# A two-layer decoder trunk on one core: the low part of two weight pairs per unit taken from DRAM twice by GpSimd's transfers

## The chip, the cores and the metric

One core of one Trainium2 chip runs the whole program in one launch. The metric is device time in microseconds (us) from start to end. Before the change the median of 3 runs is 2133.17 us (2133.06 to 2133.46). All data is float32.

## The reference

For 256 tokens of width 2048 and two layers:

```python
h = rms_norm(x, attn_norm)
proj = h @ w_in                 # columns: GLA q,k,v,gate, a rank-16 gate, attention q,k,v
o_gla = gla_chunked(...)        # gated linear attention, 8 heads
o_sb  = stick_breaking_attention(...)   # 8 heads, strictly causal
x = x + concat(o_gla, o_sb) @ w_o
hm = rms_norm(x, mlp_norm)
x = x + square(relu(hm @ w_up)) @ w_down        # hidden width 8192
```

Nearly all of the work is matrix products of the 256 tokens with float32 weights.

## The kernel before

TensorE multiplies in a rounded float32 format. To keep float32 precision each weight tile is split in two: `whi` is the weight rounded, `wlo` is what the rounding dropped. Operands are split in the same way, and a product is three matmuls of 128x512: high times `whi`, high times `wlo`, low times `whi` (`product`, L1112 to L1123).

The work of the projections is cut into **units**: 1024 output columns of one weight matrix, with 2048 input rows in eight **pairs** of 128-row blocks (0 to 7). A layer's list is `g` (gate columns), two `o`, then eight `up` and eight `down`; in between stand `iv`, `ik`, `iq`, three projections of the next layer, which also stand ahead of layer 0. 38 units are of the kinds `up`, `down`, `iv`, `ik`, `iq`. In such a unit there are three kinds of pair:

- **Fast pairs** (1, 3, 5, 6): a Strassen-like scheme, four steps of 6, 6, 6 and 3 matmuls (21 instead of 24), for which VectorE forms sums of weight blocks (`ts`, L840).
- **Plain pairs** (0, 4): two steps of 12 matmuls, each on one half tile of 128x1024. ScalarE copies `raw` to `whi` (L1008), VectorE subtracts to get `wlo` (L1012).
- **Added pairs** (2, 7): two steps of 12 matmuls. ScalarE makes `whi` (L1008) and also a rounded, negated copy `dlo` (L1018); then a transfer issued by GpSimd adds `raw` to `dlo` within SBUF (L1021), so that `dlo` holds the low part and VectorE does nothing. There are two `dlo` tiles.

All raw weights come by transfers issued on SyncE (`load`, L967 to L981) into five `raw` tiles of 1 MB that are used in turn (three named `raw`, two named `raw2`). There are five `whi` half tiles and four `wlo` half tiles, also used in turn, so the splitting runs four or five steps ahead of TensorE.

The order on TensorE, VectorE and ScalarE within these stretches is set by `Plan`: each piece of work has a length written in the code, a due time counted back from TensorE's order, and the pieces are placed by earliest due time. SyncE and GpSimd keep the order of the code. Code outside these stretches (the opening, and the attention of each layer) is ordered by the framework, which also decides where the first planned pieces stand among the code ahead of them.

At the opening, x comes in four blocks `xb`; each is turned by TensorE (L471) with the identity `ident` that GpSimd builds, scaled and split by ScalarE (L481) and VectorE (L487); then the first unit (value columns) runs with its own splitting (L575, L577) of loads at L564, and its matmuls are at L594 to L596. The attention uses the same code (L575, L594).

Of the kernel before, what the change touches and what calls it, by code (L numbers as in the profile page):

```python
# [17 lines left out]
P = 128  # L18
# [3 lines left out]
STEPS = [0, 0, 1, 1, 1, 2, 3, 1, 3, 2, 3, 3, 4, 4, 5, 5, 6, 5, 5, 6, 6, 6, 7, 7]  # L22
LOADS = [0, 1, 2, 3, 4, 5, 6, 7]
FAST = (1, 3, 5, 6)
FEWER = [0, 0, 1, 1, 1, 2, 3, 1, 3, 2, 3, 3, 4, 4, 5, 5, 6, 6, 6, 6, 7, 7], (1, 3, 6)
ADDED = (2, 7)
# [21 lines left out]
class Plan:  # L48
# [10 lines left out]
    class Piece:  # L59
        def __init__(self, engine, length, fn, deps, lag):  # L60
            self.engine, self.length, self.fn, self.lag = engine, length, fn, lag
            self.deps = deps
            self.users = []
            self.after = []
# [4 lines left out]
    def add(self, engine, length, fn, *deps, lag=0.0):  # L69
        flat = []  # L70
        for d in deps:
            flat.extend(d if isinstance(d, (list, tuple)) else [d])
        self.pieces.append(Plan.Piece(engine, length, fn, [d for d in flat if d], lag))
        return self.pieces[-1]

    def run(self):
# [25 lines left out]
        order, events, count = [], [], 0  # L102
        for p in self.pieces:
            if not p.deps:
                events.append((0.0, count, p))
                count += 1
        came = set()
        while events:
            now, _, p = heapq.heappop(events)
# [6 lines left out]
            for e in free:  # L116
                if free[e] > now + 1e-9:
                    continue
                if e in ready:
                    if not ready[e]:  # L120
                        continue
                    p = heapq.heappop(ready[e])[2]
# [6 lines left out]
                heapq.heappush(events, (free[e], count, None))  # L129
                count += 1  # L130
                for u in p.users:
# [4 lines left out]
                    if not left[u]:  # L136
                        heapq.heappush(events, (at[u], count, u))
# [9 lines left out]
def trunk_kernel(  # L147
# [59 lines left out]

    ATT = ("wg", "ident16", "mask16", "tri", "nones", "gmask", "reset", "v4", "lr", "lrT", "ha", "hh", "hl", "hA", "on", "dec", "S", "kdz", "row", "bc", "eg")
    MLP = ("whi5", "dlo", "sxh", "sx", "ts", "raw2")
# [213 lines left out]
    def forms(op, i, t, tag):  # L423

        keep = tag is None
# [16 lines left out]
        def high():  # L442
            if e:
                if keep:
# [378 lines left out]
    def ordered(l, units, hT, rst, ug, gates_t, mixed=None, ons=None):  # L823
# [11 lines left out]
        RING, LOWS, ADDS, RAWS = 5, 4, 2, 5  # L835
# [11 lines left out]
        def unit_order(u):  # L847

            kind, _, n2 = units[u]
            if kind == "g":  # L850
                return [i // 2 for i in range(8)], ()
            if kind == "o":
                pairs = ((4, 5, 6, 7, 0, 1, 2, 3), (4, 5, 6, 0, 7, 1, 2, 3))[n2]
                return [j for j in pairs for _ in range(4 if j < 2 else 2)], (0, 1)
            return FEWER if u and units[u - 1][0] == "down" and kind == "iv" else (STEPS, FAST)

        def step_banks(u, j, is_fast):
# [4 lines left out]
            if kind in BIG and j in ADDED and not by_columns(u, j):  # L862
# [24 lines left out]
        def squares(n, ss):  # L887
            return add("ACT", 2 * A1, lambda: norm_squares(n, ss), x_done[n])
# [23 lines left out]
        def made(f, got, tag_fast, first):  # L912
# [9 lines left out]
            if tag_fast:  # L922
                e = add("DVE", 1.25, lambda: part(0), first)
            b = add("ACT", A1 * (2 if tag_fast else 1), lambda: part(1), e)
            return add("DVE", 1.1 if tag_fast else V1, lambda: part(2), b)

        def turned(n, h2, m, op, key, ll, sums=False):
# [4 lines left out]
            if sums and fast(i):  # L932
                box = []
                b = add("ACT", A1, lambda: box.append(scaled()), a)
                free[m] = [b]
                return made(
                    lambda: forms(op, i, box[0], None if op is hT else "sxh"), None, True, b
# [23 lines left out]
        def load(u, i):  # L961
# [4 lines left out]
            def fn():  # L966
                if x % RAWS >= RAWS - 2:  # L967
                    box.append(tmp("raw2", [P, 2, 1024], bufs=2))
# [5 lines left out]
                if by_columns(u, i):  # L974
                    for c in range(2):
                        nc.sync.dma_start(
                            dst[:, c, :].rearrange("p (k n) -> p k n", k=2),
                            src[:, :, c * 512 : (c + 1) * 512],
                        )
                else:  # L980
                    nc.sync.dma_start(dst, src)  # L981
# [8 lines left out]
        def by_columns(u, i):  # L990

            return units[u][0] in BIG and i in ADDED and i == unit_order(u)[0][-1]
# [763 lines left out]
```

## Time and profile before

| | |
|---|---|
| median of 3 runs | 2133.17 us |
| span of the profiled execution, first to last instruction | 2131.6 us |
| TensorE busy | 2123.5 us |
| VectorE busy | 1929.5 us |
| ScalarE busy | 1535.1 us |
| GpSimd busy | 152.1 us |
| moved by transfers of SyncE (queue q1) | 407.25 MB |
| moved by transfers of GpSimd (queue q0) | 79.70 MB |

The span is 1.6 us below the median of the runs; that difference lies around the first and the last instruction. PE is TensorE, DVE VectorE, ACT ScalarE, POOL GpSimd, SP SyncE. In a timeline row the columns are start, duration, engine, line, operation, written tile <- read tiles, and in brackets how long the engine had been idle and what ended that. In a windows row the columns are the stretch, busy time of PE, PE's weight loads, DVE, ACT and POOL with counts, the granted TensorE clock, the mean busy share of the 16 DMA engines and the GB/s that they moved. A row of a DMA queue ends with the time that its packets took, as a share of 16 engines over the span.

### The profile page before, as it was taken

The numbers are of one execution on the slowest core, as the hardware profiler recorded it, in microseconds if no ns is written. First come the engines' busy times: TensorE is split into PE (matmuls) and PEld (weight loads), VectorE is DVE, ScalarE is ACT, GpSimd is POOL, SyncE is SP. The second block draws the span as 40 slices with busy tenths as digits, with TensorE's granted clock in tenths as the row PEclk, the third lists the DMA queues.
The fourth block names the chain that finished last, engine by engine and source line by source line (L and its number), as shares of the span: only waits on it lengthen the run. The fifth ranks groups of instructions, "written<-read, shape, count | busy, mean of one in ns | idle before, by whom it ended". The sixth has DMA issues, their size and how long they took to land.

```text
span 2131.6 us, 28370 instructions
## 1 busy us (share of the span) xinstructions
PE 2123.5 (100%) x10094; PEld 1768.9 (83%) x10094; DVE 1929.5 (91%) x2598; ACT 1535.1 (72%) x1989; POOL 152.1 (7%) x210
## 2 busy tenths in 40 slices
PE   9999999999999999999999999999999999999999
PEld 7888888888888888888888888888888888888887
DVE  6988779999999999999998886799999999999998
ACT  7777666777677677677777665667876776776775
POOL 0010000000000000000000100000000000000000
PEclk9999999999999999999999999999999999999999
DMA  8975355688888888878888644657888888888886
GB/s 287 265 203 182 115 198 178 217 242 264 249 247 252 249 256 249 269 237 254 238 260 252 178 138 136 201 186 219 262 234 267 245 261 250 246 254 248 254 252 178
DMA packets 156114, 488.76 MB, mean 229 GB/s; under 512 B 9690, under 2 KB 18466, under 8 KB 155972
## 3 DMA queue, kind: packets, MB, share of 16 engines
q1 hardware_dynamic: 134084, 407.25, 55.9%
q0 software_dynamic: 21888, 79.70, 19.7%
q8 instruction: 79, 1.29, 0.2%
q14 instruction: 63, 0.52, 0.1%
HBM read 405.12 MB, written 2.10 MB: 191 GB/s over the span
## 4 chain that ended last, share of the span: by engine, by line
PE 96%; DVE 2%; ACT 1%; issue 0%; DMA 0%; DVEq 0%; ACTq 0%
PE acc L594 3%; PE acc L596 3%; PE acc L595 3%; DVE wlo L1012 0%; PE ps L1693 0%; PE ps L1686 0%; DVE wlo L577 0%; PE ps L705 0%; PE ps L1643 0%; PE ps L759 0%; PE ps L723 0%; DMA dlo<-raw 0%; DVE t L1548 0%; PE ps L471 0%; PE ps L771 0%
## 5 line engine op out<-in xcount | busy, mean ns | idle before, releaser
L1008 ACT ACTIVATE whi<-raw 128x1024 fp32r<-128x1024 f32 (+1 forms) x847 | 814.9, 976 | 344.5 <-issue 48.2
L1012 DVE TENSOR_TENSOR wlo<-raw,whi 128x1024 fp32r<-128x1024 f32 (+1 forms) x695 | 757.6, 1097 | 88.3 <-ACT whi L1008 76.0
L1021 POOL DMA_DIRECT2D dlo<-raw x152 | 129.4, 852 | 1733.7 <-ACT dlo L1018 921.1
L1008 ACT ACTIVATE whi<-ts 128x1024 fp32r<-128x1024 f32 x159 | 168.6, 1060 | 80.0 <-DVE ts L840 5.8
L1012 DVE TENSOR_TENSOR wlo<-ts,whi 128x1024 fp32r<-128x1024 f32 x159 | 193.9, 1219 | 11.1 <-ACT whi L1008 8.4
L840 DVE TENSOR_TENSOR ts<-raw 128x1024 f32<-128x1024 f32 x159 | 194.0, 1220 | 2.7 <-DMA raw<-in_w_in_dram 0.9
L1018 ACT ACTIVATE dlo<-raw 128x1024 fp32r<-128x1024 f32 x152 | 155.3, 1044 | 3.6 <-PE m__2021_9487 L1122 1.7
L594 PE MATMUL acc<-whi,act 128*128 128x512 f32 (+2 forms) x384 | 141.3, 368 | 0.0
L596 PE MATMUL acc<-whi,act 128*128 128x512 f32 (+2 forms) x384 | 136.9, 356 | 0.0
L595 PE MATMUL acc<-wlo,act 128*128 128x512 f32 (+2 forms) x384 | 136.7, 356 | 0.0
L575 ACT ACTIVATE whi<-raw 128x1024 fp32r<-128x1024 f32 (+2 forms) x98 | 88.5, 908 | 63.7 <-PE acc L596 63.0
L577 DVE TENSOR_TENSOR wlo<-raw,whi 128x1024 fp32r<-128x1024 f32 (+2 forms) x98 | 100.4, 1031 | 33.2 <-ACT whi L575 33.1
L840 DVE TENSOR_TENSOR raw<-raw 128x512 f32<-128x512 f32 x159 | 109.4, 688 | 2.7
L840 DVE TENSOR_TENSOR raw<-ts,raw 128x512 f32<-128x512 f32 x159 | 108.9, 685 | 0.7
L594 PEld LDWEIGHTS acc<-whi,act 128*128 128x128 f32 x384 | 72.6, 189 | 12.3 <-issue 3.4
L596 PEld LDWEIGHTS acc<-whi,act 128*128 128x128 f32 x384 | 72.4, 189 | 10.5
L595 PEld LDWEIGHTS acc<-wlo,act 128*128 128x128 f32 x384 | 72.6, 189 | 8.9 <-DVE wlo L577 0.2
L1213 ACT ACTIVATE act<-act,st 128x512 f32<-128x512 f32 x88 | 60.3, 712 | 25.9 <-DVE act L840 25.9
L456 DVE TENSOR_TENSOR act<-t,act 128x512 fp32r<-128x512 f32 x88 | 59.8, 683 | 0.0
L452 ACT ACTIVATE act<-t 128x512 fp32r<-128x512 f32 x88 | 54.3, 621 | 0.4 <-DVE t L440 0.3
L840 DVE TENSOR_TENSOR xb<-t,xb 128x512 f32<-128x512 f32 x40 | 27.3, 682 | 0.1
L663 DVE TENSOR_REDUCE st<-t 128x4 f32<-128x512 f32 (+1 forms) x36 | 21.8, 619 | 5.7 <-ACT t L662 5.5
(3399 smaller groups left out, 5605.6 us busy)
## 6 DMA issues: line engine op xcount, KB each, us to landing
raw<-in_w_up_dram SPq DMA_DIRECT2D x112, 1024.0 KB, 6.3
raw<-in_w_down_dram SPq DMA_DIRECT2D x112, 1024.0 KB, 6.3
raw<-in_w_in_dram SPq DMA_DIRECT2D x78, 1024.0 KB, 5.5
dlo<-raw POOLq DMA_DIRECT2D x152, 512.0 KB, 6.5
raw<-in_w_o_dram SPq DMA_DIRECT2D x32, 1024.0 KB, 5.1
raw<-in_w_up_dram SPq DMA_DIRECT2D x32, 512.0 KB, 6.7
raw<-in_w_down_dram SPq DMA_DIRECT2D x32, 512.0 KB, 6.5
raw<-in_w_in_dram SPq DMA_DIRECT2D x26, 512.0 KB, 6.4
```

Of the source, the lines that this page charges most:

```text
L456: nc.vector.tensor_tensor(d[:, :, 1, :], src, f32(d[:, :, 0, :]), ALU.subtract)
L575: newest["hi"] = nc.scalar.activation(h, r, AF.Copy).ins
L577: newest["lo"] = nc.vector.tensor_tensor(lo[:, q : q + step, :width], r, f32(h), ALU.subtract).ins
L594: nc.tensor.matmul(o, xh[:, sl], whi[:, j, :width], start=first, stop=False)
L595: nc.tensor.matmul(o, xh[:, sl], wlo[:, j, :width], start=False, stop=False)
L596: st["mm"] = nc.tensor.matmul(o, xl[:, sl], whi[:, j, :width], start=False, stop=last).ins
L840: nc.vector.tensor_tensor(dst, a, b, op)
L1008: nc.scalar.activation(box["h"][:, :n], src(), AF.Copy)
L1012: nc.vector.tensor_tensor(box["l"][:, :n], src(), f32(box["h"][:, :n]), ALU.subtract)
L1018: nc.scalar.activation(box["l"], src(), AF.Copy, scale=-1.0)
L1021: nc.gpsimd.dma_start(f32(box["l"]), src(), accum_op=ALU.add)
L1213: nc.scalar.activation(box[h][:, tt, :], box[h][:, tt, :], AF.Relu if into else AF.Copy, scale=(rr if into else st["rst"])[:, tt : tt + 1],)
```

## The change

The added pairs are now 2 and 4, and an added half needs no raw tile: GpSimd issues one transfer from DRAM that rounds the weights on the way into a new tile `chi` (three of them), ScalarE makes one negated copy of `chi` in `dlo`, and GpSimd issues a second transfer from DRAM that adds the weights to `dlo`. TensorE takes `chi` in place of `whi`. The two halves of an added pair stand apart in the order of the steps, with a fast pair between them. Raw tiles are three instead of five. The `Plan` now also counts the tiles of the tag `t2`, so that a piece that takes one is placed only while enough are left.

```diff
-STEPS = [0, 0, 1, 1, 1, 2, 3, 1, 3, 2, 3, 3, 4, 4, 5, 5, 6, 5, 5, 6, 6, 6, 7, 7]
-ADDED = (2, 7)
+EACH = [0, 0, 1, 1, 1, 1, 2, 3, 3, 3, 3, 2, 5, 5, 5, 5, 4, 6, 6, 6, 6, 4, 7, 7], FAST, (2, 4)
+CAST, AHEAD_BY = 3, 1
+RING, LOWS, ADDS, RAWS = 5, 4, 2, 3
...
+        def rounded(u, j, s):
+            src = weights(u, j)[:, :, sl] if by_columns(u, j) else weights(u, j)[:, s : s + 1, :]
...
+            def high():
+                box["h"] = tmp("chi", [P, 2, 512], F32R, bufs=CAST)
+                nc.gpsimd.dma_start(flat("h"), src)
+
+            def negated():
+                box["l"] = tmp("dlo", [P, 2, 512], F32R, bufs=ADDS)
+                nc.scalar.activation(box["l"], f32(box["h"]), AF.Copy, scale=-1.0)
+
+            def add_weights():
+                nc.gpsimd.dma_start(flat("l"), src, accum_op=ALU.add)
+
+            users = [[], []]
+            h = add("POOL", 1.0, high, chi[-CAST] if len(chi) >= CAST else [], lag=LAND)
+            chi.append(users[0])
+            if len(late) >= AHEAD_BY:
+                late.pop(0)()
+            got = [box, h, None, users]
+
+            def rest():
+                m = add("ACT", A2, negated, h, dlo[-ADDS] if len(dlo) >= ADDS else [])
+                dlo.append(users[1])
+                got[2] = add("POOL", 1.0, add_weights, m, lag=ADD)
+
+            late.append(rest)
+            return got
...
-            def negated():
-                box["l"] = tmp("dlo", [P, 2, 512], F32R, bufs=ADDS)
-                nc.scalar.activation(box["l"], src(), AF.Copy, scale=-1.0)
-
-            def add_weights():
-                nc.gpsimd.dma_start(f32(box["l"]), src(), accum_op=ALU.add)
...
-            loads = LOADS if kind in BIG else list(dict.fromkeys(order))
-            raw = {j: load(u, j) for j in loads}
+            raw = {j: load(u, j) for j in dict.fromkeys(order) if j not in by_dma}
```

In the built programs TensorE has the same 9880 matmuls and VectorE the same 2600 instructions. ScalarE has 152 activations fewer (152 halves in 38 units), GpSimd has 304 transfers of 0.5 MB instead of 152, and SyncE loads 76 pairs (1 MB each) fewer.

Three places in the order of instructions. First GpSimd, from the identity at the start of the program. Before, its first transfers stand behind the identity:

```order
masks.py:197 MEMSET ident 128x128
masks.py:199 ISA
masks.py:199 AFFINE_SELECT ident<-ident 128x128
L1021 DMA dlo_457<-raw_400 128x1024
L1021 DMA dlo_467<-raw_400 128x1024
```

Now (L1032 is the rounding transfer, L1039 the adding one):

```order
masks.py:197 MEMSET ident 128x128
L1032 DMA chi_398<-in_w_in_dram 128x1024
masks.py:199 ISA
masks.py:199 AFFINE_SELECT ident<-ident 128x128
L1032 DMA chi_400<-in_w_in_dram 128x1024
L1039 DMA dlo_406<-in_w_in_dram 128x1024
L1032 DMA chi_413<-in_w_in_dram 128x1024
L1039 DMA dlo_408<-in_w_in_dram 128x1024
```

One rounding transfer stands ahead of the identity's selection and one right behind it; a third, and two adding ones, follow.

Second ScalarE at the start of the program. Before (`act_122`, `act_127` are operands of x block 0, `raw_146` the first weights):

```order
L241 ACT_TABLE_LOAD
L481 ACTIVATE act_122<-ps_109,gcol_a 128x256 x2
L481 ACTIVATE act_127<-ps_114,gcol_a 128x256 x2
L575 ACTIVATE whi_151<-raw_146 128x512 x2
L575 ACTIVATE whi_159<-raw_146 128x512 x2
```

Now (L499 is L481 of before, L593 is L575, L1036 the negated copy):

```order
L256 ACT_TABLE_LOAD
L1036 ACTIVATE dlo_406<-chi_398 128x1024
L1036 ACTIVATE dlo_408<-chi_400 128x1024
L499 ACTIVATE act_122<-ps_109,gcol_a 128x256 x2
L499 ACTIVATE act_127<-ps_114,gcol_a 128x256 x2
L593 ACTIVATE whi_151<-raw_146 128x512 x2
L593 ACTIVATE whi_159<-raw_146 128x512 x2
```

Two negated copies, each behind its rounding transfer, now stand ahead of everything else that ScalarE does.

Third ScalarE where the attention of layer 0 ends and unit `g` begins. Before (`raw_2917` is the first weight tile of `g`, `act_2896` the gates):

```order
L784 ACTIVATE act_2712<-ps_2834 128x512
L1008 ACTIVATE whi_622_2925<-raw_2917 128x1024
L662 ACTIVATE t_591_2847<-act_2712 128x512
L386 ACTIVATE st_2851<-st_2850 128x4
L387 ACTIVATE st_2851<-st_2851 128x4
L880 ACTIVATE act_2896<-acc_2610,st_393 128x512
L1008 ACTIVATE whi_2930<-raw_2917 128x1024
```

Now (L802, L680, L401, L402, L902, L1065 are L784, L662, L386, L387, L880, L1008 of before):

```order
L802 ACTIVATE act_2697<-ps_2819 128x512
L680 ACTIVATE t_585_2832<-act_2697 128x512
L401 ACTIVATE st_2836<-st_2835 128x4
L402 ACTIVATE st_2836<-st_2836 128x4
L1036 ACTIVATE dlo_2912<-chi_2904 128x1024
L1036 ACTIVATE dlo_2914<-chi_2906 128x1024
L1065 ACTIVATE whi_619_2917<-raw_2902 128x1024
L902 ACTIVATE act_2881<-acc_2595,st_393 128x512
L1065 ACTIVATE whi_2925<-raw_2902 128x1024
```

The first high part of `g` moved behind the last norm of the attention and behind two negated copies for the first `up` unit, which comes three units later. Layer 1 reads the same at this place.

More of the change, by code (lines that the diff above doesn't have):

```diff
@@ L861, in step_banks @@
                 return (1, 6), (1, 6)
-            if kind in BIG and j in ADDED and not by_columns(u, j):
+            if added(u, j) and not by_columns(u, j):
                 return ((2, 4, 3, 8),) * 2
@@ L1036, in parts @@
+            whi[-1].append(lo)
+            readers.append(lo)
             last["h"] = h
             readers.append(h)
-            return box, h, lo, [whi[-1], (dlo if by_dma else wlo)[-1]]
+            return box, h, lo, [whi[-1], wlo[-1]]
         last = {}
         sums13 = []
+        chi, late, made_halves = [], [], {}
+        every = [
+            (u, k, j, order[:k].count(j))
+            for u in range(len(units))
+            for order, _, by_dma in [unit_order(u)]
+            for k, j in enumerate(order) if j in by_dma
+        ]
@@ L1144, in sums @@
             def sums(p):
-                c = add("ACT", A1, copy, p[1])
+                c = add("ACT", A1, copy, p[1], take=1, sure=1)
                 s = [
```

200 lines of the change are left out of this document (123 added, 77 removed).

## The prediction

> **What bounds the kernel now.** First the page: busy time by engine, then the two queues.
>
> ```profile
> span 2131.6 us, 28370 instructions
> PE 2123.5 (100%) x10094; PEld 1768.9 (83%) x10094; DVE 1929.5 (91%) x2598; ACT 1535.1 (72%) x1989; POOL 152.1 (7%) x210
> q1 hardware_dynamic: 134084, 407.25, 55.9%
> q0 software_dynamic: 21888, 79.70, 19.7%
> ```
>
> TensorE is idle for 2131.6 - 2123.5 = 8.1 us in all. The windows say where that is.
>
> ```profile
> 0.00:100.00 100.00, 97.38 (x432) 79.41 (x433) 81.35 (x116) 74.77 (x112) 6.06 (x12) 1.00 0.89 283
> 500.00:600.00 100.00, 100.00 (x442) 82.80 (x442) 94.31 (x109) 68.13 (x75) 8.48 (x10) 1.00 0.87 260
> 2000.00:2132.00 132.00, 127.36 (x577) 105.12 (x575) 120.50 (x156) 91.22 (x110) 10.18 (x12) 0.99 0.75 216
> ```
>
> In the MLP (second row) TensorE never stops: 442 matmuls in 100 us, one each 0.226 us, at the full clock. 2.6 us are lost in the first 100 us, 4.6 us in the last stretch. ScalarE is busy for 68% there, VectorE for 94%. Last, TensorE's waits for what the change replaces, and the groups of it:
>
> ```profile
> PE m__79_428 L1122 <- DMA dlo<-raw: 0.3, 1, 0.3
> L1008 ACT ACTIVATE whi<-raw 128x1024 fp32r<-128x1024 f32 (+1 forms) x847 | 814.9, 976 | 344.5 <-issue 48.2
> L1018 ACT ACTIVATE dlo<-raw 128x1024 fp32r<-128x1024 f32 x152 | 155.3, 1044 | 3.6 <-PE m__2021_9487 L1122 1.7
> L1021 POOL DMA_DIRECT2D dlo<-raw x152 | 129.4, 852 | 1733.7 <-ACT dlo L1018 921.1
> ```
>
> In 152 added halves TensorE waited once, for 0.3 us. So the gain is capped: the 152 removed ScalarE copies of 0.976 us are 148 us of an engine on which TensorE does not wait, and are worth nothing. The matmuls are the same in number and kind. What remains is the 0.3 us, and whatever the new order costs.
>
> **The added halves in the MLP: no cost.** How long the new transfers take is bounded by rows of the two queues. q1, plain loads, needs 55.9% x 2131.6 / 407.25 = 2.93 us of all 16 engines per MB, so 1.53 us per half tile (0.524 MB). q0, adding transfers, needs 19.7% x 2131.6 / 79.70 = 5.27, so 2.76 us. Before shows no rounding transfer. It reads one stream, as a plain load does, while an adding one reads two, so I take 1.53 us and keep 2.76 as the other end. An adding transfer is taken at 2.76 whether its source is SBUF or DRAM.
>
> ```profile
> DMA to landing us min/median/max: 4.5/6.5/11.8
> raw<-in_w_up_dram SPq DMA_DIRECT2D x112, 1024.0 KB, 6.3
> ```
>
> The first row is the adding transfers (issue to landing), the second the raw loads. There are two `dlo` tiles, so the negation of a half waits until TensorE has finished the half before the last. In the new order the shortest stretch from there to use is four steps of a fast pair, one added half, four steps: 21 + 12 + 21 = 54 matmuls, 12.2 us, twice in each of 38 units. In it lie the negation (1.04), the landing (6.5) and the rounding transfer of the next half, released by the same matmul and ahead in GpSimd's queue (1.5 to 2.8): 9.1 to 10.3 us. 2 us are left, so the cost is nothing. Without that cover each us later would cost 76 us. Three raw tiles are enough too: the shortest reuse, from a fast pair 6 to the next pair 1, is 81 matmuls or 18.3 us from the start of pair 6, which holds the last conversion (about 1.5), the landing (6.3) and the first sums and splits of pair 1 (about 4). All 16 engines were busy for 55.9 + 19.7 = 75.6% of the span; 79.7 MB move from q1 (-10.9%) to q0 (+10.9 to +19.7%), which gives 76 to 84%. VectorE has the same work, and between two added halves (54 matmuls less 12, 24 where pairs 7 and 0 meet) it is spread no worse than before, so again nothing.
>
> **The opening: +6 us.** The chain of the first us, the timelines of POOL, SP, ACT and PE in it, and the windows:
>
> ```profile
> 0.82 3.20 DMA xb<-in_x_dram
> 4.07 1.97 PE ps L471 x8
> ```
>
> ```profile
> 1.10 0.29 POOL masks.py:199 TENSOR_SCALAR_AFFINE_SELECT ident<-ident 128x128 f32<-128x128 f32 x1
> 2.32 1.85 SPq L564 DMA_DIRECT2D raw<-in_w_in_dram  x4
> 4.21 0.43 SPq L356 DMA_DIRECT2D xb<-in_x_dram  x1
> 6.54 1.57 ACT L481 ACTIVATE act<-ps,gcol_a 128x256 fp32r<-128x256 f32 x4 [4.44 <-DVE gcol_a L319]
> 7.98 2.37 ACT L575 ACTIVATE whi<-raw 128x512 fp32r<-128x512 f32 x4
> 12.40 0.82 PE L471 MATMUL ps<-ident,xb 128*128 128x128 f32 x6
> ```
>
> ```profile
> 2.00:4.00 2.00, 1.40 (x7) 1.00 (x5) 0.00 (x0) 0.10 (x1) 0.00 (x0) 1.00 0.91 273
> 4.00:8.00 4.00, 3.93 (x18) 3.54 (x19) 0.78 (x3) 1.46 (x5) 0.00 (x0) 1.00 0.87 219
> 8.00:12.00 4.00, 4.00 (x17) 3.32 (x16) 3.57 (x7) 3.03 (x7) 0.00 (x0) 1.00 1.04 394
> 26.00:33.00 7.00, 7.00 (x32) 5.82 (x31) 4.84 (x8) 5.22 (x13) 0.00 (x0) 1.00 1.01 382
> ```
>
> The DMA engines are full from 2 us to 33 us, so what is put in costs its own engine time to what stands behind it. Put in are two rounding transfers at about 1.1 and 2.4 us, beside x block 0 (landed at 4.02). ScalarE's first two instructions now wait for them; as each negated copy ends, GpSimd issues an adding transfer, and a third rounding one between. All this stands in time ahead of x block 1, which TensorE turns at 12.40. Its engine time: 3 x 1.53 + 2 x 2.76 = 10.1 us (13.8 with the other end). Two things take off: the engines' idle share from 2 to 8 us, 0.09 x 2 + 0.13 x 4 = 0.7 us, and the slack of block 1. Ahead of and with block 1 go 0.52 MB of x, 1.05 MB of weights and 0.52 MB, 2.1 MB; at 273, 219 and 394 GB/s these are in at 9.7 us, 2.7 us before 12.40. So 10.1 - 0.7 - 2.7 = 6.7 us, or 10.4 us. I take 6, since part of the last adding transfer falls behind block 1. From below: if the queues left x alone, ScalarE would still wait for the second rounding transfer, 2.4 + 4.5 (the quickest landing) + 1.04 = 7.9 against the start at 6.54: +1.4. The identity that comes 0.85 us later is covered by x. After block 1 the loads have more room: the early loads into `raw2` are gone.
>
> **The ends of the attentions: +2.2 us.** ScalarE, VectorE and TensorE in layer 0, and the chain in layer 1:
>
> ```profile
> 284.64 1.05 ACT L1008 ACTIVATE whi<-raw 128x1024 fp32r<-128x1024 f32 x1
> 288.03 0.21 ACT L387 ACTIVATE st<-st 128x4 f32<-128x4 f32 x1
> ```
>
> ```profile
> 285.73 1.23 DVE L1012 TENSOR_TENSOR wlo<-raw,whi 128x1024 fp32r<-128x1024 f32 x1 [2.02 <-ACT whi L1008]
> 286.87 0.68 DVE L663 TENSOR_REDUCE st<-t 128x4 f32<-128x512 f32 x1
> ```
>
> ```profile
> 289.63 0.39 PE L1121 MATMUL m__629_2942<-whi,act 128*128 128x512 f32 x1
> 289.86 0.39 PE L1122 MATMUL m__629_2942<-wlo,act 128*128 128x512 f32 x1
> ```
>
> ```profile
> 1347.97 0.69 ACT act L880
> 1348.65 0.96 ACT whi L1008
> 1349.63 1.24 DVE wlo L1012
> 1350.91 0.50 PE m__2660_12490 L1122
> ```
>
> Before, the first high part of `g` was made at 284.64, 5 us before use. Now it stands behind the last norm (288.03) and two negations. The norm itself comes some 1.4 us earlier, since the copy and the subtraction no longer stand ahead of it: about 286.8. Two negations end at 288.8 (one starts 0.95 to 1.0 us after the other), `whi` at 289.8, `wlo` 1.23 us later at 291.1, and the matmul due at 289.86 starts 1.25 us late. By then the two rounding transfers have landed: the last tile that GpSimd waits for is free near 279.3, 9 us before. In layer 1 the same, less a wait of some 0.2 us that was there (last row). 2 x 1.25 - 0.3 = 2.2 us. If the norm gains nothing, 2.7 us each, 5.4; if ScalarE catches up half, 1.
>
> **Sum.** 6 + 2.2 - 0.3 (the one wait for `dlo`) = +7.9 us on the span of 2131.6, 2139.5; with the 1.6 us by which the median lies above it, **2141 us**.
>
> **The rivals.**
> 1. *x keeps its pace* (not slower). The queue of SyncE is served as if alone, the rounding transfers fit in what is idle, and only ScalarE's wait is left: 1.4 + 1 - 0.3 = +2.1, 2135 us. It decides as soon as block 1 is delayed by less than its 2.7 us of slack. For it: the engines idle 0.7 us there, and block 1 is early. Against: the full engines from 8 us on. The Trainium skill, DMA: Bandwidth & Descriptors (Queues, rings and completion order), says that each engine takes the queues that have work in turn, packet by packet. By that rule x does not go first and +6 stands; by strict precedence of SyncE's queue it would be +1.4. No view quoted here shows two full queues at once. 15%.
> 2. *The sums land too late in the MLP.* 12.2 us are to be enough; the slowest landing before was 11.8 us, and with 1.04 and a rounding transfer ahead this would be 14.4. From 10 us landing on, TensorE waits in 76 places: half a us each is +38, 2179 us. For it: DMA busy 0.87 before, 0.9 and more then. Against: median 6.5, two added transfers were often close together before too. 12%.
> 3. *GpSimd holds up VectorE.* If each of the 152 new issues (0.852 us) held VectorE, which is busy for 94%, up to 129 us would be lost, 2270 us. VectorE's subtraction without any transfer of GpSimd, and amid ten of them:
>
> ```profile
> L577 DVE TENSOR_TENSOR wlo<-raw,whi 128x1024 fp32r<-128x1024 f32 x6 | 7.3, 1224 | 2.2 <-ACT whi L575 2.1
> L1012 DVE TENSOR_TENSOR wlo<-raw,whi 128x1024 fp32r<-128x1024 f32 x31 | 37.7, 1219 | 4.3 <-ACT whi L1008 3.8
> ```
>
> 1224 ns up to 39 us, 1219 ns from 500 to 600 us: no hold. 2%. The Trainium skill, SBUF — State Buffer (Who interferes with whom), says that a VectorE instruction with two SBUF inputs contends with a GpSimd instruction that reads SBUF and not with one that only writes; the trace agrees.
> 4. *It is faster after all*, by more than half of the 8.1 us of idle time: 2%. That the change does not do what it says is excluded by the counts of the built program.
>
> **How the numbers follow.** 0.2% (4.3 us) is about what a measurement of this kernel can tell from no change. My case has 69%, 2136 to 2149 (1.4 to 10.4, 1 to 5.4, -0.3). Rival 1 gives "same", rivals 2 and 3 and my case "slower": 2, 15 and 83 in 100. The range takes in rival 1 and a mild form of rival 2 (0.1 us in each of the 76 places), 2135 to 2156.
>
> **What would show it.** In the changed profile: the first matmul of L612 to L614 (L594 to L596 of before) about 3 us later than 8.9 and the turn of x block 1 near 18 us instead of 12.40; ScalarE's first activation a negation that waits for a transfer; the first `wlo` of `g` behind two negations at both ends of the attention; TensorE at 100.00 in a window of the MLP, DMA share 0.85 to 0.95. A TensorE busy share under 99% in the MLP would prove me wrong by rival 2; a start as early as before by rival 1.

## The result, and the profile after

The changed kernel takes 2149.25 us (median of 4 runs, 2145.61 to 2152.23); the kernel before, run beside it, 2133.28 us (2133.06 to 2133.46). The ratio is 1.0075, 95% interval 1.0061 to 1.0089: slower by 16 us. The forecast was 2141, range 2135 to 2156. Beside the median the spread has changed: 0.4 us before, 6.6 us now.

The head of the page of the changed kernel, with the row of GpSimd's queue and of its transfers (columns of the last three: count, KB each, median us from issue to landing):

```profile
span 2149.6 us, 28212 instructions
...
PE 2128.7 (99%) x10094; PEld 1768.9 (82%) x10094; DVE 1920.2 (89%) x2598; ACT 1399.6 (65%) x1837; POOL 235.3 (11%) x362
...
q0 software_dynamic: 43776, 159.40, 31.4%
...
chi<-in_w_up_dram POOLq DMA_DIRECT2D x64, 512.0 KB, 7.0
dlo<-in_w_up_dram POOLq DMA_DIRECT2D x64, 512.0 KB, 9.3
...
dlo<-in_w_down_dram POOLq DMA_DIRECT2D x64, 512.0 KB, 10.3
```

ScalarE works 135 us less than before (1535.1 to 1399.6) and TensorE still bounds. The numbers to watch are those of the adding transfers: a sum now lands 9.3 to 10.3 us after its issue; before it was 6.5.

To see where the 18.0 us of span came from, I compare when the n-th of the 10,094 matmuls starts in either trace (the profile holds 214 more than the 9880 counted in the built programs, the same number in both kernels); the growth of the difference over a stretch is what the stretch lost. For the changed kernel:

| matmuls | stage | lost, us | forecast |
|---|---|---|---|
| 1 to 100 | opening | +7.9 | +6 |
| 100 to 600 | first three units | +1.3 | -0.3 |
| 1400 to 1700, 6400 to 6700 | ends of the two attentions | +0.9, +0.9 | +2.2 |
| 1700 to 5400, 6700 to 9800 | `o` and MLP of both layers | +4.0, +3.4 | 0 |
| last 300 | end | -0.5 | 0 |

The rest is 0.0; the sum is 17.9. TensorE's waits in the changed kernel (matmul, what it waited for, us, times, longest):

```profile
PE acc L612 <- ACT whi L593: 2.6, 1, 2.6
PE ps L562 <- POOL ident masks.py:199: 2.5, 1, 2.5
PE ps L333 <- DMA t<-in_attn_norm_dram: 1.9, 1, 1.9
PE ps L489 <- DMA xb<-in_x_dram: 1.4, 1, 1.4
PE m__1060_5037 L1198 <- DMA dlo<-in_w_down_dram: 1.4, 1, 1.4
PE m__1365_6475 L1198 <- DMA dlo<-in_w_down_dram: 1.3, 1, 1.3
PE m__3055_14492 L1198 <- DMA dlo<-in_w_down_dram: 1.3, 1, 1.3
...
PE m__2619_12388 L1198 <- DVE wlo L1069: 0.8, 1, 0.8
PE m__626_2935 L1198 <- DVE wlo L1069: 0.8, 1, 0.8
```

The first four are the opening, the `dlo` rows are sums that land late in the MLP, the last two are the ends of the attentions. Each wait is named; none says yet which part of the change makes it.

**The opening.** ScalarE's first instructions:

```profile
0.82 1.28 ACT L256 ACT_TABLE_LOAD   x1 [0.82 <-PEq L1817]
8.19 1.06 ACT L1036 ACTIVATE dlo<-chi 128x1024 fp32r<-128x1024 f32 x1 [6.08 <-DMA chi<-in_w_in_dram]
10.91 1.06 ACT L1036 ACTIVATE dlo<-chi 128x1024 fp32r<-128x1024 f32 x1 [1.66 <-DMA chi<-in_w_in_dram]
11.87 1.55 ACT L499 ACTIVATE act<-ps,gcol_a 128x256 fp32r<-128x256 f32 x4
```

The operands of x block 0 (L499) begin at 11.87 instead of 6.54 us, behind two negated copies that wait for their rounding transfers. TensorE in the same stretch:

```profile
8.41 3.03 PE L562 MATMUL ps<-ident 128*128 128x128 f32 x13
13.99 0.80 PE L612 MATMUL acc<-whi,act 128*128 128x512 f32 x1 [2.55 <-ACT whi L593]
...
16.17 0.63 PE L613 MATMUL acc<-wlo,act 128*128 128x512 f32 x1
16.59 0.63 PE L614 MATMUL acc<-whi,act 128*128 128x512 f32 x1
...
18.22 0.40 PE L613 MATMUL acc<-wlo,act 128*128 128x512 f32 x1
18.46 0.39 PE L614 MATMUL acc<-whi,act 128*128 128x512 f32 x1
...
23.90 1.09 PE L489 MATMUL ps<-ident,xb 128*128 128x128 f32 x8 [1.41 <-DMA xb<-in_x_dram]
```

The first real matmul starts at 13.99 instead of 8.90 (5.1 us). The ones after it follow each other at 0.43 us until 17.45 and at 0.23 to 0.24 later (1.2 us lost), and x block 2 comes late (1.6 us).

**An end of an attention**, layer 0: ScalarE, VectorE, TensorE.

```profile
295.99 1.99 ACT L1036 ACTIVATE dlo<-chi 128x1024 fp32r<-128x1024 f32 x2
297.88 1.04 ACT L1065 ACTIVATE whi<-raw 128x1024 fp32r<-128x1024 f32 x1
```

```profile
298.96 1.23 DVE L1069 TENSOR_TENSOR wlo<-raw,whi 128x1024 fp32r<-128x1024 f32 x1 [1.56 <-ACT whi L1065]
```

```profile
298.98 0.50 PE L1197 MATMUL m__626_2935<-whi,act 128*128 128x512 f32 x1
300.24 0.50 PE L1198 MATMUL m__626_2935<-wlo,act 128*128 128x512 f32 x1 [0.76 <-DVE wlo L1069]
```

Two negated copies, the first high part, the low part, and the matmul with `wlo` starts 1.26 us after the one ahead of it, where 0.23 is due.

**A late sum in the MLP**, a `down` unit of layer 0: GpSimd, ScalarE, TensorE.

```profile
551.04 0.55 POOL L1032 DMA_DIRECT2D chi<-in_w_down_dram  x1 [16.64 <-PE m__1067_5068 L1199]
552.48 0.85 POOL L1039 DMA_DIRECT2D dlo<-in_w_down_dram  x1 [0.89 <-ACT dlo L1036]
```

```profile
551.15 1.04 ACT L1036 ACTIVATE dlo<-chi 128x1024 fp32r<-128x1024 f32 x1
```

```profile
562.81 0.39 PE L1197 MATMUL m__1060_5037<-chi,act 128*128 128x512 f32 x1
564.56 0.50 PE L1198 MATMUL m__1060_5037<-dlo,act 128*128 128x512 f32 x1 [1.36 <-DMA dlo<-in_w_down_dram]
```

The tile for the sum came free at 550.3, when the half two before it was used up. The copy starts at 551.15, the adding transfer is issued at 552.48, right behind a rounding transfer, lands 12.0 us later at 564.5, and TensorE wanted it at 563.0.

The same intervals for all halves used between 320 and 1200 us (75 or 76 in a trace; the tile is "free" when the matmul behind its last reader starts, and "room" is from there to the first matmul that reads the new sum, with TensorE's wait included; us):

| kernel | room, least / median | free to copy, median | issue to landing, median / most | landing to use, least |
|---|---|---|---|---|
| before | 12.7 / 20.2 | 4.6 | 6.5 / 10.0 | 1.9 |
| changed | 12.7 / 23.6 | 0.6 | 9.75 / 12.6 | 0.0 |
| e3 (sum first) | 12.7 / 23.6 | 4.7 | 8.3 / 10.5 | 0.0 |
| e9 (4 and 3 tiles) | 20.2 / 31.1 | 0.2 | 9.2 / 13.2 | 8.4 |
| e10 (even halves) | 14.7 / 18.5 | 0.2 | 8.2 / 11.2 | 4.6 |

From copy to issue it is 1.35 us in all of them. In the changed kernel about half of the rooms (37 of 75) are 12.7 to 14.4 us and half 23 us and more, since with halves at steps 6, 11, 16 and 21 of 24 two of the four follow the half before last by only two fast pairs and one half. The kernel before had rooms of 12.7 to 14.5 us too, 18 of 76, but no landing over 10.0 us in this stretch. In a room of 12.7 us the medians fit, 0.6 + 1.35 + 9.75 = 11.7 us; a landing of over some 11 us does not. In the eight places from 320 us on where TensorE waited for a sum by 0.1 us or more, the copy's delay, 1.35 us and a landing of 10.7 to 12.0 us add up to more than the room.

### The profile page after: what moved, and what is told of

Same layout as the page of the kernel before. It is cut to its first block, busy times and chain, and to the rows that moved or that the text cites. A ratio compares the mean times of both kernels' runs of the same rounds, so it can differ in the third digit from the quotient of the medians.

```text
span 2149.6 us, 28212 instructions
## 1 busy us (share of the span) xinstructions
PE 2128.7 (99%) x10094; PEld 1768.9 (82%) x10094; DVE 1920.2 (89%) x2598; ACT 1399.6 (65%) x1837; POOL 235.3 (11%) x362
## 4 chain that ended last, share of the span: by engine, by line
PE 46%; issue 44%; POOL 5%; DMA 2%; DVE 1%; ACT 1%; POOLq 0%
POOL dlo L1039 3%; PE acc L612 2%; PE acc L614 2%; PE acc L613 2%; POOL chi L1032 2%; DMA dlo<-in_w_down_dram 2%; DMA dlo<-in_w_in_dram 1%; DVE wlo L595 0%; DMA chi<-in_w_in_dram 0%; PE ps L723 0%; PE ps L1779 0%; PE ps L777 0%; PE ps L1729 0%; PE ps L1772 0%; PE ps L741 0%
## 5 line engine op out<-in xcount | busy, mean ns | idle before, releaser
L1065 ACT ACTIVATE whi<-raw 128x1024 fp32r<-128x1024 f32 (+1 forms) x695 | 652.3, 958 | 328.8 <-DVE raw L857 175.2
L1036 ACT ACTIVATE dlo<-chi 128x1024 fp32r<-128x1024 f32 x152 | 160.4, 1056 | 127.2 <-DMA chi<-in_w_down_dram 17.7
L1065 ACT ACTIVATE whi<-ts 128x1024 fp32r<-128x1024 f32 x159 | 168.5, 1060 | 71.1 <-DVE ts L857 41.9
L857 DVE TENSOR_TENSOR ts<-raw 128x1024 f32<-128x1024 f32 x159 | 193.5, 1217 | 5.7 <-DMA raw<-in_w_down_dram 5.2
L1069 DVE TENSOR_TENSOR wlo<-ts,whi 128x1024 fp32r<-128x1024 f32 x159 | 193.5, 1217 | 0.3 <-PE m__631_2940 L1198 0.2
L593 ACT ACTIVATE whi<-raw 128x1024 fp32r<-128x1024 f32 (+2 forms) x98 | 88.2, 906 | 64.6 <-PE acc L614 64.1
L1032 POOL DMA_DIRECT2D chi<-in_w_up_dram x64 | 35.5, 555 | 778.0 <-PE m__2815_13371 L1199 142.1
L1032 POOL DMA_DIRECT2D chi<-in_w_down_dram x64 | 35.5, 555 | 525.8 <-PE m__2985_14157 L1199 34.7
L1039 POOL DMA_DIRECT2D dlo<-in_w_down_dram x64 | 54.8, 856 | 56.8 <-ACT dlo L1036 54.4
L1039 POOL DMA_DIRECT2D dlo<-in_w_up_dram x64 | 54.9, 857 | 53.2 <-ACT dlo L1036 51.5
## 6 DMA issues: line engine op xcount, KB each, us to landing
dlo<-in_w_down_dram POOLq DMA_DIRECT2D x64, 512.0 KB, 10.3
```

What stands on the lines that cost most here:

```text
L593: newest["hi"] = nc.scalar.activation(h, r, AF.Copy).ins
L857: nc.vector.tensor_tensor(dst, a, b, op)
L1032: nc.gpsimd.dma_start(flat("h"), src)
L1036: nc.scalar.activation(box["l"], f32(box["h"]), AF.Copy, scale=-1.0)
L1039: nc.gpsimd.dma_start(flat("l"), src, accum_op=ALU.add)
L1065: nc.scalar.activation(box["h"][:, :n], src(), AF.Copy)
```

## The experiments

Theory: three separate places cost the time: ScalarE standing at negated copies that come too early in its order (opening, ends); transfers beside x (opening); sums with too little room (MLP). Rivals: it is contention everywhere, or the new transfers themselves (their source, their order) are too slow. Results by stage, in the columns of the table above (us lost against the kernel before; "ends" are both together, "MLP" both layers):

| kernel | opening | first units | ends | MLP | span | median of runs |
|---|---|---|---|---|---|---|
| changed | +7.9 | +1.3 | +1.8 | +7.4 | +18.0 | 2149.25 |
| e1 copies behind | +2.6 | +2.6 | 0.0 | +10.0 | +15.9 | 2148.65 |
| e2 and transfers behind x | -0.9 | +4.2 | 0.0 | +9.5 | +13.9 | 2147.95 |
| e3 sum first | +6.5 | +1.9 | 0.0 | +14.9 | +24.1 | 2154.46 |
| e4 three sums | +8.0 | +4.3 | +1.8 | +86.3 | +103.2 | 2235.20 |
| e5 sum from the chip | +7.4 | +0.6 | +1.8 | +17.2 | +26.5 | 2159.39 |
| e6 four and three tiles | -0.5 | +4.2 | +9.8 | +1.7 | +15.1 | 2148.79 |
| e7 planned two ahead | -0.4 | +5.2 | +9.4 | +2.8 | +17.1 | 2150.39 (one run) |
| e8 first unit mixed | -0.4 | +1.4 | 0.0 | +12.2 | +12.8 | 2146.12 (one run) |
| e9 first high part | -0.6 | +1.3 | 0.0 | +1.5 | +1.8 | 2135.57 |
| e10 even halves | +7.5 | +0.1 | +1.7 | 0.0 | +8.8 | 2142.41 |
| e11 even, behind | -0.7 | +4.2 | 0.0 | 0.0 | +3.6 | 2137.29 |
| e12 even, first unit mixed | -0.5 | +1.3 | 0.0 | 0.0 | +0.4 | 2133.78 |

The stretches that are not in the table (between the attentions, and the last 300 matmuls) make -0.5 to +2.6 us, so a row's stages do not add up to its span. Beside these runs the kernel before ran at 2132.78 to 2133.01 (medians).

### e1: negated copies behind the first high parts

```
-                m = add("ACT", A2, negated, h, dlo[-ADDS] if len(dlo) >= ADDS else [])
+                m = add("ACT", A2, negated, h, dlo[-ADDS] if len(dlo) >= ADDS else first_h)
...
+            if len(first_h) < 2:
+                first_h.append(h)
```

> The first two negated copies of each layer are put behind the first high part of the layer on ScalarE; the rounding transfers start as early as before. Theory (the opening's 7.9 us and the 0.9 us at each end of the attention come from ScalarE standing at a negated copy that waits, with the sums that follow it too early): the matmul before the first unit of the attention no longer waits 1.3 us at either end (-1.8 us), and the opening loses half of its 7.9 us, since two adding transfers and ScalarE's wait go but three rounding transfers stay ahead of x: about -6 us against the changed kernel's 2149, 2143. Rival (the opening is all contention of the transfers, ScalarE's place counts for nothing): the opening keeps over 6 us and only the two ends go, 2146.

The waits at the two ends are gone, and 5.3 us of the opening. ScalarE there:

```profile
6.94 1.57 ACT L499 ACTIVATE act<-ps,gcol_a 128x256 fp32r<-128x256 f32 x4 [4.83 <-DVE gcol_a L334]
8.65 0.63 ACT L593 ACTIVATE whi<-raw 128x512 fp32r<-128x512 f32 x1
```

It starts at 6.94, close to the 6.54 of before the change. So most of the opening was ScalarE's order and the two sums that follow it, not the rounding transfers. The median of the runs moved by 0.6 us only: in the executions that were profiled the MLP lost 10.0 us here and 7.4 there, and the first units 1.3 us more. Which stage had gained could be read from the stages alone.

### e2: and the first rounding transfers behind x

```
+                if behind_x:
+                    nc.gpsimd.tensor_copy(box["h"][:, 0, :1], xb[3][:, 0, :1])
...
+            behind_x = l < 0 and len(chi) < CAST
```

> As e1, and the first three rounding transfers wait until x block 3 has landed (a one-column copy from it into their tiles by GpSimd stands ahead of them). Theory (contention with x is the other half of the opening): the opening costs 0 to 1 us in place of 7.9, the profile's first matmuls stand as in the kernel before, total -9 us, 2140. Rival (the opening is late for fewer tiles of raw weights, not for the transfers): the opening stays 3 us late or more, 2143 as e1.

The opening is 0.9 us shorter than in the kernel before; the other 3.5 us were transfers beside x and the identity's later selection (x block 1 lands at 10.79 us, in e1 at 14.47). The rest of the expectation missed: of the 8.8 us that the opening gave back against the changed kernel, the first units took 2.8, and the MLP kept its waits for sums (9.5 us). The span fell by 4.1, the medians, with runs from 2144.29 to 2152.78, by 1.3.

### e3: the adding transfer ahead of the next rounding transfer

```
-            h = add("POOL", 1.0, high, chi[-CAST] if len(chi) >= CAST else [], lag=LAND)
-            chi.append(users[0])
             if len(late) >= AHEAD_BY:
                 late.pop(0)()
+            h = add("POOL", 1.0, high, chi[-CAST] if len(chi) >= CAST else [], lag=LAND)
+            chi.append(users[0])
```

> GpSimd issues the adding transfer of a half ahead of the rounding transfer of the next one; nothing else is changed. Theory A (the sums land late in the MLP because each stands in GpSimd's queue behind a rounding transfer that was issued a us earlier): the median landing of the sums falls from 9 to 10 us to 6.5 to 8, and the 7.4 us that TensorE waits for sums in the MLP fall to under 2: 2144. Theory B (the room of 12.2 us between two sums is too short whatever the order, and the rounding transfers now come late to their negated copies): waits stay at 5 us or more, 2149.

The median landing falls from 9.75 to 8.3 us, not to the 6.5 to 8 of theory A. But the planner now puts the negated copy a median of 4.7 us after its tile is free (0.6 in the changed kernel), 2.1 to 4.2 us in the places where TensorE waits, and the waits double. Neither theory came true as I put it: the landing is shorter, and the time is longer since the copy starts later in a room that is as short as before. Whether the 1.4 us are the order in the queue stays open, since e10 below gains as much with the order unchanged.

### e4: three tiles for the sums

```
-RING, LOWS, ADDS, RAWS = 5, 4, 2, 3
+RING, LOWS, ADDS, RAWS = 5, 4, 3, 3
```

> Three tiles for the sums in place of two; nothing else is changed. Theory (a sum has only the 12.2 us from the end of the half two before it, and 12 us is what a slow landing takes): with some 8 us more no matmul of the MLP waits for a sum, -7.4 us in the profile, the runs lie closer together than 2145.6 to 2152.2, 2142. Rival (the transfers are late because the DMA engines as a whole can't carry them in the busy stretches): the waits move a little and stay, 2147 or more.

86 us lost in the MLP. ScalarE's waits between 400 and 1200 us:

```profile
ACT dlo L1036 <- DMA chi<-in_w_up_dram: 57.5, 16, 6.1
ACT dlo L1036 <- DMA chi<-in_w_down_dram: 45.2, 18, 7.0
...
ACT dlo L1036 <- DMA chi<-in_w_in_dram: 10.8, 4, 5.0
```

113.5 us, where the changed kernel has 26.7. Sums were no longer short of room, yet the third tile let the planner put each copy earlier on ScalarE, up to where its rounding transfer had not landed yet, and everything behind it on ScalarE stood (in the MLP TensorE's longest single wait is for `whi`, and the most time goes to 53 waits for the tile `t` of L1317, which ScalarE makes as well). GpSimd's order turned as well in 103 of 152 places: the adding transfer, which waits for its copy, stands there ahead of the next rounding transfer. A ring of one resource was lengthened without the one that feeds it.

### e5: the sum's source on the chip

```
-                nc.gpsimd.dma_start(flat("l"), src, accum_op=ALU.add)
+                nc.gpsimd.dma_start(f32(box["l"]), f32(box["h"]), accum_op=ALU.add)
```

> The adding transfer takes its source from the rounded tile on the chip in place of the weights in DRAM, so the lower parts of the added halves come out as zero: the output leaves out these corrections, the count and size of transfers stay. The kernel before also added from the chip, with a median landing of 6.5 us. Theory (DRAM as the source makes the sums late): the median landing falls from 9 to 10 us to 6.5 to 7.5 and the 7.4 us of waits for sums in the MLP fall under 1: 2142. Rival (the rounding transfer ahead in the queue and the raw loads beside it make them late): landing 8.5 or more, waits stay at 5 us or more: 2148.

The median landing is 9.7 us as with DRAM, so the second read from DRAM is not what makes a sum late, as the rival said. The waits even grew to 17 us and the runs spread from 2153.07 to 2166.71. Some 3.4 us of that are the half clock behind two waits of 2.4 us (see the last section); why the waits themselves are longer stays open.

### e6 and e7: four rounded tiles, three for the sums

```
-CAST, AHEAD_BY = 3, 1
-RING, LOWS, ADDS, RAWS = 5, 4, 2, 3
+CAST, AHEAD_BY = 4, 1
+RING, LOWS, ADDS, RAWS = 4, 4, 3, 3
```

(on e2; e7 has `AHEAD_BY = 2`)

> As e2, with four rounded tiles and three for the sums, and four high-part tiles in place of five to make room. Theory (e4 lost 103 us because the third tile for the sums moved each negated copy ahead to where its rounding transfer hadn't landed, and ScalarE stood there; with a fourth rounded tile the transfer has a half more to land): ScalarE waits under 20 us for rounded tiles from 400 to 1200 us in place of 113, no matmul waits for a sum, 2136 to 2139. Rival (four high-part tiles are too few, or ScalarE waits as in e4): 2150 or more.

> As e6, with rounding transfers planned two halves ahead in place of one. GpSimd's order of transfers differs only in a few places, so the same as e6 within 3 us if the tiles set the times; if the plan's order does, some 5 us or more apart.

The MLP is down to 1.7 us, none of TensorE's listed waits is for a sum, and ScalarE waits 17.9 us for rounded tiles from 400 to 1200 us (under 20 expected). So the explanation of e4 holds: with a fourth rounded tile the third sum does good. The rival was right on the total, though. TensorE's longest waits in e6:

```profile
PE m__76_424 L1202 <- ACT whi L1068: 2.6, 1, 2.6
PE m__2613_12378 L1202 <- ACT whi L1068: 2.4, 1, 2.4
PE m__620_2925 L1202 <- ACT whi L1068: 2.3, 1, 2.3
```

One at each layer's start, 4.9 us lost at each of the two ends and as much at the first unit: the fifth high-part tile, given up for room, was the one in which the first high part was made ahead of the end of the attention (e9 tests this). e7 is 1.6 us slower in its one run, within the 3 us expected if the tiles set the times.

### e8: the first unit's steps mixed

```
-OWN = {}
+OWN = {("iv", 0): ([0, 0, 1, 1, 1, 3, 2, 1, 3, 5, 3, 2, 3, 5, 5, 6, 4, 5, 6, 6, 7, 4, 6, 7], FAST, (2, 4))}
```

> As e2, but in the first unit the steps of fast pairs are mixed with their neighbours as in the kernel before, with the halves at the same four steps. Theory (from 44 to 94 us TensorE loses 2.1 us in e2 since VectorE has 9 us of work in each fast pair of 4.8 us there, and four such steps in a row outrun its ring of low parts): the 2.1 us fall under 1. Rival (the third raw tile, missing now, sets VectorE back): they stay at 2 or grow.

From matmul 190 to 400 (44 to 94 us) the loss falls from 1.5 to 0.2 us, from 100 to 190 it rises from 0.65 to 1.1: 2.15 to 1.3 in all, above the 1 that was expected. The order of the fast pairs is a part of it and not the whole.

### e9: the first high part in a rounded tile

```
-        before = [add("PE", 12 * MM, None) for _ in range(RING)]
+        before = [add("PE", 12 * MM, None) for _ in range(RING + 1)]
...
-            if RING > 4 and len(whi) % RING == 0:
-                return lambda: tmp("whi5", [P, 2, 512], F32R, bufs=1)
+            if len(whi) == RING + 1:
+                return lambda: tmp("chi", [P, 2, 512], F32R, bufs=CAST)
...
-            h = add("ACT", A2 if n == 2 else A1, high, deps, whi[-RING], last.get("h"))
+            h = add("ACT", A2 if n == 2 else A1, high, deps, whi[-RING - (len(whi) < 2 * RING + 2)], last.get("h"))
```

(on e6, with the first unit of e8)

> As e6 and e8 together, and the first high part of each layer takes a rounded tile in place of the fifth high-part tile that e6 had given up. Theory (e6's only new loss is 4.9 us at the start of each of the three layers, where the first high part waited until the attention gave back one of the four high-part tiles): the three waits go, -14.7 us against e6; no matmul of the MLP waits for a sum; the span is 2131 to 2134, the time 2133 to 2136. Rival (four high-part tiles are too few all over the first unit): some 4 us stay at each start, 2145.

All the starts are back, 13 us gained against e6, and span and time lie where they were expected. The ratio to the kernel before is 1.0011, interval 1.0002 to 1.0020: 2.6 us slower still. In the profiled execution the MLP loses 1.5 us, though no matmul there waits for a sum.

### e10, e11, e12: evenly spaced halves

```
-EACH = [0, 0, 1, 1, 1, 1, 2, 3, 3, 3, 3, 2, 5, 5, 5, 5, 4, 6, 6, 6, 6, 4, 7, 7], FAST, (2, 4)
+EACH = [0, 0, 1, 1, 2, 1, 1, 3, 3, 3, 2, 3, 5, 5, 5, 5, 4, 6, 6, 6, 6, 7, 4, 7], FAST, (2, 4)
```

(and the shorter order in the same way; e10 on the changed kernel, e11 on e2, e12 is e11 with the first unit of e8)

> The changed kernel with the four halves of a unit at steps 4, 10, 16 and 22 of 24 in place of 6, 11, 16 and 21, so that from the end of one half to the start of the next but one there are some 18 us everywhere in place of 12.7 in half of the places and 23 to 25 in the others. Theory (only the short room makes TensorE wait; the landing of 9.7 us median, 12.6 at most, and 1.9 us ahead of it fit into 18): the waits for sums in the MLP fall from 7.4 us to under 1, 2142; the opening and the two ends stay as they are. Rival (the sums land as late as the room allows, or the fast pairs now split make other waits): over 5 us of waits stay, 2147 or more.

> The even halves of e10 with the opening and the ends of e2 (negated copies behind the first high parts, the first rounding transfers behind x block 3). Theory (the three losses, opening, ends, sums in the MLP, are all that the change costs): the span is 2131 to 2135, the time 2133 to 2137, as close to the kernel before as its own waits in the first unit (some 2 us) allow. Rival (something else is still slow): 2140 or more.

> As e11, with the first unit alone in the mixed order of e8 (halves at steps 6, 11, 16 and 21 there). Theory (of the 3.5 us that e11 keeps, 2.6 are the first sum, which is wanted at step 4 of the first unit, 9 us after its transfer is issued, and the rest VectorE's load in the first unit): the first sum is in time, 1.1 and 0.2 us stay in the first unit, the span is 0.2 to 0.8 us above that of the kernel before, 2133.2 to 2133.8, and the ratio is 1.000 within its interval. Rival (the step from the mixed to the even order makes the second unit's first sum late): 2135 or more.

e10 alone, with the changed kernel's tiles, sources and queue order, takes the MLP's 7.4 us to 0.0, and its runs lie within 0.4 us (2142.16 to 2142.58; ratio 1.0043, interval 1.0029 to 1.0056). So more room is enough. The landings are also shorter in e10 (8.2 us), but that is not needed for it: even the changed kernel's slowest landing of 12.6 us would fit its least room, 0.2 + 1.35 + 12.6 = 14.2 of 14.7 us. Faster landings may be enough as well: the kernel before has the same least room and no late sum in the MLP. e11 comes out at 2137.29, just above the 2133 to 2137 that were expected; its only wait for a sum is the first one:

```profile
PE m__79_430 L1203 <- DMA dlo<-in_w_in_dram: 2.6, 1, 2.6
```

e12 removes it. Its page and all of TensorE's waits:

```profile
span 2132.0 us, 28175 instructions
...
PE 2123.7 (100%) x10094; PEld 1769.0 (83%) x10094; DVE 1924.1 (90%) x2598; ACT 1398.8 (66%) x1837; POOL 236.6 (11%) x365
```

```profile
PE ps L562 <- POOL ident masks.py:199: 1.4, 1, 1.4
PE ps L723 <- DVE act L686: 1.1, 2, 0.5
PE m__77_428 L1203 <- DVE wlo L1072: 0.5, 1, 0.5
PE ps L489 <- DMA xb<-in_x_dram: 0.5, 1, 0.5
PE m__75_426 L1203 <- DVE wlo L1072: 0.2, 1, 0.2
```

2133.78 us, ratio 1.0004, interval 0.9995 to 1.0013: no difference from the kernel before. With all three places mended, and the first unit in the old order, the double reading is free, and brings nothing, since what it saves (135 us of ScalarE, 80 MB of SyncE's loads) is not what bounds: TensorE is busy for 2123.7 of 2132.0 us.

## Why the prediction was right, and where it was not

The direction, the range and two of the places were right; the size was half of the measured one (+7.9 against +18.0 of span). One sum in it is off by a little: the lower ends of the case, 1.4 + 1 - 0.3, give 2135 and not 2136.

- **The ends of the attentions (+2.2): right.** The mechanism shows row by row: the matmul with the first `wlo` comes 1.26 us after the one ahead of it where 0.23 is due, so it is 1.0 us late where 1.25 us were forecast, and e1 takes that away by the order of ScalarE alone. Both ends together make 1.8 since a loss of 0.3 to 0.4 us that the kernel before had at a later low part went at both, and the forecast took it off in layer 1 alone. The rounding transfers were issued 6.9 us ahead of their copies (289.12 and 295.99 us) and, as forecast, did not hold them up.
- **The opening (+6): the size nearly right by chance, its parts exchanged.** The forecast gave 6 of 6.7 us to transfers ahead of x block 1 and took ScalarE's standing as a lower bound of 1.4 us, with the second rounding transfer landing at 6.9 us. It landed at 10.9. x block 1 was turned at 18.69, as forecast (near 18), but it had landed at 13.61: the third rounding transfer and the two adding ones landed at 17.9 to 23.2, beside block 2 (23.86) and not ahead of block 1. By e1 and e2 ScalarE's standing and the sums behind it are 5.3 us, the transfers and the identity 3.5; together they are more than 7.9, as the opening without both is 0.9 us shorter than before.
- **Rival 1, that x keeps its pace: wrong.** With ScalarE free (e1) the first 100 matmuls are still 2.6 us late, against -0.9 in e2 where the rounding transfers wait for x, and x block 1 lands 3.7 us later than there. The rule of the Trainium skill, DMA: Bandwidth & Descriptors (Queues, rings and completion order), that was weighed there, that an engine takes the queues with work in turn, fits this.
- **The MLP (0): the step that failed.** The forecast let 12.2 us of room cover 9.1 to 10.3 us that are needed: the negation, a landing of 6.5 us (the median before) and the rounding transfer ahead (1.5 to 2.8). The room was right (12.7 with the matmuls ahead of the first that reads the sum), and the engine time too (1.7 us of all 16 engines for a rounding transfer where 1.53 was taken, from the two pages' shares of queue q0, if an adding one takes what it took before). The median landing came out longer, 9.75 us with the rounding transfer ahead where 8.0 to 9.3 was allowed for; yet 11.7 us of medians still fit. What failed is that medians were set against the room: the slowest landing between 320 and 1200 us is 12.6 us where it was 10.0 before, and 0.2 + 1.35 + 12.6 = 14.2 us does not fit into 12.7. The forecast had this sum (14.4) in rival 2 and gave it 12%.
- **Why the landings grew: open.** Reading from DRAM is none of it (e5). Turning the order (e3) takes 1.4 us off the median, but so does even spacing with the order as it is (e10, 1.5). In e3, 13 of the 74 adding transfers issued between 320 and 1200 us had no rounding transfer in flight beside them and landed in 5.2 to 5.6 us, while the 49 with one on either side took a median of 8.7; but the raw loads moved a median of 43 GB/s beside the first and 149 beside the others, so the two are not separated.
- **Rival 2, mild.** What came is its mild form, put at 0.1 us in each of 76 places (7.6 us), which is why the range held. In the profiled execution it is 7.4 us, in some ten places of up to 1.5 us and not in all; that the two figures agree is luck. TensorE was busy for 99.65% from 400 to 1200 us, so the sign that was set for the full rival (under 99%) did not show. An average landing that fits says little: the tail decides. It may also give the changed kernel's runs their spread of 6.6 us, as the four runs of e10, without late sums, lie within 0.4 us.
- **The wait for `dlo` (-0.3), and the first units.** That wait went (0.6 us with the spacing behind it, matmul 194), and with it one of 0.4 us for VectorE (188). But from matmul 190 to 400 TensorE loses 2.1 us to low parts that VectorE makes, where it lost 0.6, and at matmul 476, in the second unit, 0.7 us to a sum that landed late: +1.3 in all. The forecast put VectorE at nothing, as its work is the same and spread no worse; in the first unit, with the steps of a fast pair in a row, that was wrong. e8 shows the order to be part of it, and e10, which has no late sum there, has 0.1.
- **Rival 3, that GpSimd's issues hold VectorE: wrong, as forecast.** The subtraction on `ts` takes 1217 ns on average with 304 transfers issued, and took 1219 ns before with 152 (second row):

```profile
L1069 DVE TENSOR_TENSOR wlo<-ts,whi 128x1024 fp32r<-128x1024 f32 x159 | 193.5, 1217 | 0.3 <-PE m__631_2940 L1198 0.2
L1012 DVE TENSOR_TENSOR wlo<-ts,whi 128x1024 fp32r<-128x1024 f32 x159 | 193.9, 1219 | 11.1 <-ACT whi L1008 8.4
```

## What to carry to other kernels

When work is moved to a queue of transfers, write down for each buffer the room from its release to its next use, place by place, and set it against the slowest landing rather than the median; uneven spacing can make half of the places short where the average has plenty. When buffers are added to one stage of a chain, the stage that feeds it needs them too, and an engine that works in order must not meet a waiting instruction ahead of work that is due. If the bounding engine is already busy for all but 0.4% of the span, relieving the others can at best cost nothing.

## What the runs showed of the hardware

- In the changed kernel TensorE's first matmuls of 512 columns started up to 0.43 us apart until 17.45 us, 3.5 us after the first, and 0.23 us apart from then on, while the granted clock stands at 1.00 in that window; in the kernel before, whose opening has shorter waits, the spacing was 0.23 from 10.35 us on, 1.5 us after the first. Part of the price of a wait in the opening is thus paid behind it: 1.2 us here. The Trainium skill, TensorE: Matmul & The Clock Gate (Part 1: The HAM clock gate (the "warmup" mystery)), says that an array that has been idle runs at half its clock until some 3.4 us of work have passed, with 426.7 ns between matmuls of 512 columns; the trace agrees (0.42 to 0.43 us, 3.5 us of matmuls behind two waits). In the MLP a wait of 1.4 us was followed by starts 0.34 and then 0.23 us apart.
- Behind longer waits outside the opening the granted clock itself shows it. In e2 a matmul of the MLP waited 2.3 us for a sum, until 892.71; windows ahead of, in and behind the slow stretch:

```profile
889.00:892.68 3.68, 1.38 (x7) 0.80 (x5) 2.52 (x3) 1.95 (x3) 0.00 (x0) 1.00 1.03 299
892.68:896.09 3.41, 3.38 (x8) 2.71 (x9) 0.00 (x0) 0.00 (x0) 0.00 (x0) 0.50 1.04 316
896.09:899.00 2.91, 2.91 (x14) 2.39 (x14) 0.71 (x1) 1.55 (x2) 1.33 (x2) 1.00 0.74 251
```

  The clock is 0.50 for 3.41 us, matmuls start 0.43 us apart there, and this costs 1.7 us on top of the wait. In all traces of this case, from 30 us on, none of TensorE's 16 waits of 1.3 to 1.9 us was followed by such a stretch (3.41 us, sometimes 6.83) within 3 us, and 12 of the 14 waits of 1.9 to 2.9 us were. So a sum that is late by over 2 us mostly costs 1.7 us more than its lateness, and the 4.9 us that e6 lost at each end hold such a stretch.
- A transfer of GpSimd that is added into a tile lands no sooner when its source is on the chip (9.7 us) than when it is in DRAM (9.3 to 10.3 us).
